# Two-layer hybrid trunk on one core: small gather, scatter and one-hot products placed inside the branch blocks, some GpSimd weight splits moved to VectorE, the second tile's input norm rewritten

## The chip, the cores and the metric

One core of one Trainium2 chip runs the whole program. The metric is device microseconds (us) of one execution, the median of several runs. Lower is better. Everything below stands in us unless it says otherwise.

## The reference, cut to what matters

Two layers over 256 tokens of width 1024, all fp32. Each layer is a token mixer and a channel mixer, each followed by a layer norm of `alpha * x + f(x)`. The channel mixer of the first layer is a dense SwiGLU, that of the second a mixture of eight experts:

```python
x = layer_norm(x, ln_emb_g, ln_emb_b)
for l in range(2):
    x = layer_norm(DN_ALPHA * x + hybrid_mixer(x, w_in[l], ...), ln1_g[l], ln1_b[l])
    f = swiglu(x, ...) if l == 0 else moe_swiglu(x, router, w_gate, w_up, w_down)
    x = layer_norm(DN_ALPHA * x + f, ln2_g[l], ln2_b[l])

def moe_swiglu(x, w_router, w_gate, w_up, w_down):   # w_gate, w_up: 8 x 1024 x 3584, w_down: 8 x 3584 x 1024
    top_v, top_i = lax.top_k(xt @ w_router, 2)
    top_w = jax.nn.softmax(top_v, axis=-1)
    gates = jnp.sum(one_hot(top_i, 8) * top_w[..., None], axis=1)
    for e in range(8):
        y = y + gates[:, e:e + 1] * swiglu(xt, w_gate[e], w_up[e], w_down[e])
```

## The kernel before, in words

**Weights.** Every weight arrives as fp32 and is split on the chip into a high part `whi` (a ScalarE copy, L151) and a low part `wlo` (the difference, L152, on VectorE or, where a list says so, on GpSimd). A product of two fp32 matrices is then three TensorE products, high by high, high by low, low by high (`mm3`, L161 to L163). `split` (L147) makes one such pair; `hold_splits` (L155) fills a list that says for each of the next splits on which engine its low part runs and after which instruction it may be issued.

**Start.** The 256 tokens are two tiles of 128. `norm` (L1242) does the input layer norm of a tile in four VectorE instructions of 128x512 (two at L1247, two at L1250). The first tile is normed and transposed, then the second by `second` and `third`, which hang on the split numbers in R1 = (0, 1) and on START, the list of splits whose low part is on GpSimd. NEXT is the same list for the second layer's mixer.

**Experts** (`moe`, L637). An expert takes only the tokens routed to it: a matrix of ones and zeros `pm` picks them, at most 128 rows per expert. The gather products `gx` (L741) multiply the token tiles by `pm` and are copied to `xg` in high and low parts; experts go in pairs. The result of an expert goes back by scatter products `sc` (L993, L994), which VectorE adds to the rows `r` (L999). Between the two stand `gsb` (L800, L802), which turn `pm` over and pick the gate weights, copied by ScalarE to `gs` and `pTm` (L805, L806).

The hidden width 3584 is cut into seven chunks of 512. One iteration is one (expert e, chunk m) and has three stages on TensorE: gate (`eg`, 24 products of 128x512), up (`eg`, 24) and, for the chunk before, down (`y`, 24). After the gate stage the last chunk's hidden values are transposed (`ht`, L166) and copied to `wk`, high part by ScalarE (L943), low part by VectorE (L945); the down stage multiplies `wk` by the down weights. Each stage's weight, 1024x512, is split in two pieces of 128x2048, so there are six pairs of `whi` and `wlo` in one iteration.

**Two ways through a stage.** Expert 0 is static. For experts 1 to 7 each stage is an If (`either`, L853): with more than 64 tokens the heavy way runs 24 products, with at most 64 the light way packs high and low parts side by side and runs 16 (with a fold, L863). With this input, experts 3, 5 and 6 are heavy and 1, 2, 4 and 7 are light. The branch stands on TensorE, ScalarE, VectorE and GpSimd alike; what is called between two Ifs stands between the two branches in each engine's order.

**Chores.** The gather of the next pair (eight pieces of four products), the one-hot products of a pair (two pieces of eight) and the scatter of an expert (four pieces of two) are called chores here. They lie in a list; `point` (L824) runs one if it is due, three times per iteration: after gate, after up, after down. The chore's products are issued there and its copies or sum are put off with `defer(CHORE_N, ...)`, CHORE_N = 4, that is by two splits of 2048 columns; `msplit` (L830) calls what has come due after each split. Each chore takes one PSUM bank out of a pool of four, `acc`, two of which hold `y`.

A scheduler in the framework lays out each engine's order within a stretch between branches, so chores called at different points may come to stand next to each other.

```python
def point():
    points[0] += 1
    if chores and chores[0][0] <= points[0]:
        chores.pop(0)[1]()
...
with tc.If(few[e] == 0) as cmp:
    heavy()
with cmp.Else():
    light()
```

**Start of the experts.** The router's logits are sorted to the two best (L699 to L712), counted (`pc`, L716) and turned into positions (`posm`, L721) and `pm` (L729). Three of the first splits of expert 0 have their low part on GpSimd (the `hold_splits` line in `gather`).

Of the kernel before, what the change touches and what calls it, by code (L numbers as in the profile page):

```python
# [18 lines left out]
P = 128  # L19
# [18 lines left out]
R1, R2 = (0, 1), (0, 5)  # L38
WF = 6
HBUF = 3  # L40
NEXT = (True, False, True, False)
# [45 lines left out]
def trunk(ctx: ExitStack, tc: tile.TileContext, x, consts, mconsts, vecs, lnrows, w_in, w_uq, w_ukv, w_o,  # L87
# [59 lines left out]
    def split(src, n, lo_eng=None, to=None):  # L147
        hi, lo = to or [spl[0].tile([P, 1024], F32R, tag=t, name=t) for t in ("whi", "wlo")]
        ins, eng = plan.pop(0) if plan else ((), lo_eng)
        with after(*ins):  # L150
            last[0] = nc.scalar.copy(hi[:, :n], src)  # L151
            last[1] = (eng or nc.vector).tensor_tensor(lo[:, :n], src, hi.bitcast(F32)[:, :n], ALU.subtract)  # L152
        return hi, lo

    def hold_splits(*steps):  # L155
        plan.clear()
        for ins, eng, n in steps:
            plan.extend([(ins, eng)] * n)
# [478 lines left out]
    def moe(pool, raws2, raws3, r, gb, rw):  # L637
# [87 lines left out]
        def gather(pr):  # L725
# [5 lines left out]
            if pr == 0:  # L731
                hold_splits(((), None, 2), ((pw,), nc.gpsimd, 2), ((i1, pw), nc.gpsimd, 1), ((i1, ip), None, 3))
            xgs = [pool.tile([P, KD, P, 2], F32R, tag="xg", name="xg", bufs=3) for j in range(2)]

            def half_part(k2, hl, n=0):
                src = (xth, xtl)[hl]
                b = bank(acc, "gx")
                for kk in range(2):
                    k = 2 * k2 + kk
                    for tt in range(2):  # L740
                        nc.tensor.matmul(b[:, kk * 256:(kk + 1) * 256], src[:, tt, k * P:(k + 1) * P], pm[:, tt, :],  # L741
                                         start=(kk == 0 and tt == 0), stop=(kk == 1 and tt == 1))
# [10 lines left out]
                defer(n, copies)  # L753

            def part(k2):
                for hl in range(2):
                    half_part(k2, hl)
# [28 lines left out]
        def gather2(pr, pm):  # L786
# [10 lines left out]
            def one(j):  # L797
                b = bank(acc, "gsb")
                for tt in range(2):
                    nc.tensor.matmul(b[:, 256:264], pmf[:, tt, j * P:(j + 1) * P], gates[:, tt, :], start=(tt == 0), stop=False)  # L800
                for tt in range(2):
                    nc.tensor.matmul(b[:, tt * P:(tt + 1) * P], pmf[:, tt, j * P:(j + 1) * P], ident, start=False, stop=(tt == 1))  # L802
# [5 lines left out]
                defer(CHORE_N, copies)  # L808
# [15 lines left out]
        def point():  # L824
            points[0] += 1
            if chores and chores[0][0] <= points[0]:
                chores.pop(0)[1]()


        def msplit(raw, o, halves=False, before=None):  # L830
            t = [spl[0].tile([P, 2048], F32R, tag=x, name=x) for x in ("whi", "wlo")]
            n = 1024 if halves else 2048
            for c in range(0, 2048, n):
# [4 lines left out]
                for q in list(later):  # L838
                    q[0] -= n // 1024
                    if q[0] <= 0:  # L840
                        later.remove(q)
                        q[1]()
# [10 lines left out]
        def either(e, heavy, light):  # L853
            if few[e] is None:
                return heavy()
            with tc.If(few[e] == 0) as cmp:
                heavy()
            with cmp.Else():
                light()

# [4 lines left out]
        def gate_up(e, m, xg, part=None, mid=None):  # L865
# [12 lines left out]
            for g, w in enumerate((e_gate, e_up)):  # L878
# [25 lines left out]
                else:  # L904
                    for q in range(2):
                        four(q)
                        heavy(range(4 * q, 4 * q + 4))
                if dyn:
# [18 lines left out]
            point()  # L927
# [483 lines left out]
```

## Time and profile before

| what | value |
| --- | --- |
| median of 3 runs | 1468.8 us (1468.71 to 1469.89) |
| the profiled execution's own time | 1468.16 us |
| its span in the trace | 1466.0 us |
| TensorE busy | 1359.3 us (93%), 6927 products |
| VectorE busy | 1176.5 us (80%) |
| ScalarE busy | 997.0 us (68%) |
| GpSimd busy | 78.4 us (5%) |
| mean granted TensorE clock | 0.987 |
| weights and tokens read | 426.76 MB |

The span runs from the first to the last instruction that the trace shows; the execution's own time is 2.16 us more. Busy time counts an engine as busy while an instruction is on it; TensorE's products overlap, so two neighbours' durations add up to more than they take. "Idle before" in a row is the time in which that engine did nothing ahead of the row, with the instruction that ended the wait. The experts take the span from about 491 to 1443 us.

### The profile page before, as it was taken

The numbers are of one execution on the slowest core, as the hardware profiler recorded it, in microseconds if no ns is written. First come the engines' busy times: TensorE is split into PE (matmuls) and PEld (weight loads), VectorE is DVE, ScalarE is ACT, GpSimd is POOL, SyncE is SP. The second block draws the span as 40 slices with busy tenths as digits, with TensorE's granted clock in tenths as the row PEclk, the third lists the DMA queues.
The fourth block names the chain that finished last, engine by engine and source line by source line (L and its number), as shares of the span: only waits on it lengthen the run. The fifth ranks groups of instructions, "written<-read, shape, count | busy, mean of one in ns | idle before, by whom it ended". The sixth has DMA issues, their size and how long they took to land. (4 is left out here: it accounts for less than half of the span.)

```text
span 1466.0 us, 18597 instructions
## 1 busy us (share of the span) xinstructions
PE 1359.3 (93%) x6927; PEld 1118.0 (76%) x6927; DVE 1176.5 (80%) x1256; ACT 997.0 (68%) x1073; POOL 78.4 (5%) x113
## 2 busy tenths in 40 slices
PE   7999999999999899988989999998999999999895
PEld 6987999998987688766666677866677787787663
DVE  6577655557677788899999987898998788788996
ACT  3564444444565677788978877787986777778794
POOL 3011000004102100000000000000000000000101
PEclk9999999999999999999999999999999999999998
DMA  6733555544534699999999998899998799899980
GB/s 264 276 135 115 189 186 186 188 157 153 194 116 201 231 339 356 375 365 349 420 406 369 419 382 323 325 367 348 407 419 342 295 357 357 311 358 389 357 363 30
DMA packets 63513, 429.46 MB, mean 293 GB/s; under 512 B 7058, under 2 KB 7570, under 8 KB 15268
## 3 DMA queue, kind: packets, MB, share of 16 engines
q1 hardware_dynamic: 63364, 427.81, 76.4%
q8 instruction: 81, 1.33, 0.4%
q14 instruction: 36, 0.29, 0.1%
q0 software_dynamic: 32, 0.03, 0.0%
HBM read 426.76 MB, written 1.05 MB: 292 GB/s over the span
## 5 line engine op out<-in xcount | busy, mean ns | idle before, releaser
L152 DVE TENSOR_TENSOR wlo<-raw,whi 128x2048 fp32r<-128x2048 f32 (+4 forms) x475 | 911.0, 1939 | 158.3 <-ACT whi L151 156.7
L151 ACT CAST whi<-raw 128x2048 fp32r<-128x2048 f32 (+4 forms) x482 | 771.0, 1619 | 250.5 <-PE gu L585 44.0
L898 PE MATMUL eg<-wlo,xg 128*128 128x512 f32 x448 | 185.6, 414 | 22.1 <-DVE wlo L152 19.0
L162 PE MATMUL eg<-wlo,xg 128*128 128x512 f32 x448 | 178.0, 397 | 0.8 <-DVE wlo L152 0.3
L161 PE MATMUL eg<-whi,xg 128*128 128x512 f32 x448 | 178.6, 399 | 0.0
L897 PE MATMUL eg<-whi,xg 128*128 128x512 f32 x448 | 178.4, 398 | 0.0
L163 PE MATMUL eg<-whi,xg 128*128 128x512 f32 x448 | 176.6, 394 | 0.0
L898 PEld LDWEIGHTS eg<-wlo,xg 128*128 128x128 f32 x448 | 84.4, 188 | 70.4 <-DVE wlo L152 54.9
L971 PE MATMUL y<-wlo,wk 128*128 128x512 f32 x224 | 94.2, 421 | 17.0 <-DVE wlo L152 15.8
L162 PEld LDWEIGHTS eg<-wlo,xg 128*128 128x128 f32 x448 | 86.9, 194 | 21.5 <-DVE wlo L152 5.4
L163 PEld LDWEIGHTS eg<-whi,xg 128*128 128x128 f32 x448 | 86.7, 194 | 17.3
L584 PE MATMUL gu<-xhi,whi 128*128 128x256 f32 x352 | 99.8, 283 | 0.1
L585 PE MATMUL gu<-xlo,whi 128*128 128x256 f32 x352 | 99.7, 283 | 0.2 <-DVE xlo L224 0.2
L161 PEld LDWEIGHTS eg<-whi,xg 128*128 128x128 f32 x448 | 86.9, 194 | 16.7
L586 PE MATMUL gu<-xhi,wlo 128*128 128x256 f32 x352 | 99.6, 283 | 0.0
L897 PEld LDWEIGHTS eg<-whi,xg 128*128 128x128 f32 x448 | 84.9, 189 | 15.0 <-ACT whi L151 0.5
L971 PE MATMUL y<-whi,wk 128*128 128x512 f32 x224 | 90.3, 403 | 3.6 <-DVE wk L945 1.5
L162 PE MATMUL y<-wlo,wk 128*128 128x512 f32 x224 | 88.0, 393 | 3.6 <-DVE wlo L152 3.4
L161 PE MATMUL y<-whi,wk 128*128 128x512 f32 x224 | 87.5, 392 | 0.4 <-ACT hh L919 0.4
L163 PE MATMUL y<-whi,wk 128*128 128x512 f32 x224 | 87.3, 390 | 0.0
L971 PEld LDWEIGHTS y<-wlo,wk 128*128 128x128 f32 x224 | 44.1, 197 | 42.7 <-DVE wlo L152 36.0
L584 PEld LDWEIGHTS gu<-xhi,whi 128*128 128x128 f32 x352 | 67.6, 192 | 0.7 <-DVE xlo L224 0.3
(313 smaller groups left out, 2111.8 us busy)
## 6 DMA issues: line engine op xcount, KB each, us to landing
raw<-in_e_gate SPq DMA_DIRECT2D x112, 1024.0 KB, 7.1
raw<-in_e_up SPq DMA_DIRECT2D x110, 1024.0 KB, 7.2
raw<-in_e_down SPq DMA_DIRECT2D x108, 1024.0 KB, 7.4
raw<-in_ffn_gu SPq DMA_DIRECT2D x22, 1024.0 KB, 4.8
raw<-in_ffn_dn SPq DMA_DIRECT2D x11, 1024.0 KB, 4.7
raw<-in_w_in SPq DMA_DIRECT2D x10, 960.0 KB, 4.7
raw<-in_w_o SPq DMA_DIRECT2D x8, 1024.0 KB, 6.7
gb<-in_lnrows SPq DMA_DIRECT2D x8, 512.0 KB, 5.3
```

Of the source, the lines that this page charges most:

```text
L151: last[0] = nc.scalar.copy(hi[:, :n], src)
L152: last[1] = (eng or nc.vector).tensor_tensor(lo[:, :n], src, hi.bitcast(F32)[:, :n], ALU.subtract)
L161: nc.tensor.matmul(o, ahi, bhi, start=start, stop=False)
L162: nc.tensor.matmul(o, ahi, blo, start=False, stop=False)
L163: return nc.tensor.matmul(o, alo, bhi, start=False, stop=stop)
L584: nc.tensor.matmul(o, hi[:, cs], xhi[:, k, :], start=(g == 0 and k == 0), stop=False)
L585: nc.tensor.matmul(o, hi[:, cs], xlo[:, k, :], start=False, stop=False)
L586: nc.tensor.matmul(o, lo[:, cs], xhi[:, k, :], start=False, stop=(g == 1 and k == 7))
L897: nc.tensor.matmul(bs[g], x2, sp[k // 4][0][:, cs], start=(k == 0), stop=False)
L898: nc.tensor.matmul(bs[g], x2, sp[k // 4][1][:, cs], start=False, stop=(k == 7))
L971: nc.tensor.matmul(yb[n], h2, sp[j // 2][i][:, j % 2 * D + n * 512:j % 2 * D + n * 512 + 512], start=(m == 0 and j == 0 and i == 0), stop= ...
```

## The change

Five things change.

1. A chore now returns its products and its follow-up apart. `step` takes the place of `point`; `either` calls it once per stage and runs the products at the end of the heavy block and at the end of the light block, and puts off the follow-up by CHORE_N behind the If. Expert 0, which has no If, runs them at the end of each stage.
2. What has come due after a split is now issued after that split's two instructions (`after(last[0], last[1])` in `msplit`). Scatter chores are due two steps later, not three.
3. At the start of the experts the three splits whose low part was on GpSimd go to VectorE, and are issued after `pm`.
4. At the start of the kernel the second tile's norm is one ScalarE instruction (x * rstd - mean * rstd), one VectorE product with the scale and one VectorE sum with the shift, each 128x1024, in place of four VectorE instructions of 128x512; one small GpSimd instruction gives -mean * rstd. R1 goes from (0, 1) to (0, 3), so the second of these steps comes three splits later.
5. NEXT loses its first entry: one split of 128x832 of the second layer's mixer goes from GpSimd to VectorE.

```diff
@@ -35,10 +35,10 @@
 START = (False, True, False, True)
-R1, R2 = (0, 1), (0, 5)
+R1, R2 = (0, 3), (0, 5)
 WF = 6
 HBUF = 3
-NEXT = (True, False, True, False)
+NEXT = (False, False, True, False)
 R3 = (0, 7)
@@ -146,16 +146,17 @@
         hi, lo = to or [spl[0].tile([P, 1024], F32R, tag=t, name=t) for t in ("whi", "wlo")]
-        ins, eng = plan.pop(0) if plan else ((), lo_eng)
+        ins, eng, late = plan.pop(0) if plan else ((), lo_eng, ())
         with after(*ins):
             last[0] = nc.scalar.copy(hi[:, :n], src)
+        with after(*ins, *late):
             last[1] = (eng or nc.vector).tensor_tensor(lo[:, :n], src, hi.bitcast(F32)[:, :n], ALU.subtract)
         return hi, lo
 
     def hold_splits(*steps):
         plan.clear()
-        for ins, eng, n in steps:
-            plan.extend([(ins, eng)] * n)
+        for ins, eng, n, *late in steps:
+            plan.extend([(ins, eng, late)] * n)
 
@@ -729,17 +730,19 @@
             if pr == 0:
-                hold_splits(((), None, 2), ((pw,), nc.gpsimd, 2), ((i1, pw), nc.gpsimd, 1), ((i1, ip), None, 3))
+                hold_splits(((), None, 2), ((i1,), None, 3, ip), ((i1, ip), None, 3))
             xgs = [pool.tile([P, KD, P, 2], F32R, tag="xg", name="xg", bufs=3) for j in range(2)]
 
-            def half_part(k2, hl, n=0):
+            def half_part(k2, hl):
                 src = (xth, xtl)[hl]
                 b = bank(acc, "gx")
-                for kk in range(2):
-                    k = 2 * k2 + kk
-                    for tt in range(2):
-                        nc.tensor.matmul(b[:, kk * 256:(kk + 1) * 256], src[:, tt, k * P:(k + 1) * P], pm[:, tt, :],
-                                         start=(kk == 0 and tt == 0), stop=(kk == 1 and tt == 1))
+
+                def products():
+                    for kk in range(2):
+                        k = 2 * k2 + kk
+                        for tt in range(2):
+                            nc.tensor.matmul(b[:, kk * 256:(kk + 1) * 256], src[:, tt, k * P:(k + 1) * P], pm[:, tt, :],
+                                             start=(kk == 0 and tt == 0), stop=(kk == 1 and tt == 1))
 
@@ -750,11 +753,12 @@
 
-                defer(n, copies)
+                return products, copies
 
             def part(k2):
                 for hl in range(2):
-                    half_part(k2, hl)
+                    for f in half_part(k2, hl):
+                        f()
 
@@ -821,10 +827,11 @@
 
-        def point():
+        def step():
             points[0] += 1
             if chores and chores[0][0] <= points[0]:
-                chores.pop(0)[1]()
+                return chores.pop(0)[1]()
+            return (lambda: None), (lambda: None)
 
@@ -839,7 +846,8 @@
                     q[0] -= n // 1024
                     if q[0] <= 0:
                         later.remove(q)
-                        q[1]()
+                        with after(last[0], last[1]):
+                            q[1]()
             return t
@@ -851,12 +859,14 @@
 
 
         def either(e, heavy, light):
-            if few[e] is None:
-                return heavy()
+            products, then = step()
             with tc.If(few[e] == 0) as cmp:
                 heavy()
+                products()
             with cmp.Else():
                 light()
+                products()
+            defer(CHORE_N, then)
 
@@ -905,6 +915,9 @@
                         heavy(range(4 * q, 4 * q + 4))
+                    products, then = step()
+                    products()
+                    defer(CHORE_N, then)
                 if dyn:
@@ -924,7 +937,6 @@
 
-            point()
             if e == 0 and m == 0:
@@ -990,13 +1005,19 @@
             b = bank(acc, "sc")
-            nc.tensor.matmul(b, pT[:, tt, :], y[0], start=True, stop=False)
-            nc.tensor.matmul(b, pT[:, tt, :], y[1], start=False, stop=True)
-            if last:
-                ln_sum(ya[tt], ya[tt], {n: b}, fsums[tt], 1.0, (n,))
-            else:
-                cs = slice(n * 512, (n + 1) * 512)
-                defer(CHORE_N, lambda: nc.vector.tensor_tensor(ya[tt][:, cs], ya[tt][:, cs], b, ALU.add))
+
+            def products():
+                nc.tensor.matmul(b, pT[:, tt, :], y[0], start=True, stop=False)
+                nc.tensor.matmul(b, pT[:, tt, :], y[1], start=False, stop=True)
+
+            def add():
+                if last:
+                    ln_sum(ya[tt], ya[tt], {n: b}, fsums[tt], 1.0, (n,))
+                else:
+                    cs = slice(n * 512, (n + 1) * 512)
+                    nc.vector.tensor_tensor(ya[tt][:, cs], ya[tt][:, cs], b, ALU.add)
+
+            return products, add
 
@@ -1107,14 +1129,14 @@
                         for tt in range(2):
-                            chores.append((points[0] + 3, lambda n=n, tt=tt: scatter(n, tt, ys[n], pT)))
+                            chores.append((points[0] + 2, lambda n=n, tt=tt: scatter(n, tt, ys[n], pT)))
 
         def prepare_scatter(pr):
             one = []
 
             def first():
                 one.append(gather2(pr, half[pr][0]))
-                one[0](0)
+                return one[0](0)
 
@@ -1136,7 +1158,6 @@
                 def mid():
-                    point()
                     if prev is not None:
@@ -1153,7 +1174,6 @@
                     finish(*prev[:2], ht[0], fold_up, e, hook if (e, m) == LAST else None)
-                point()
                 if m == 3 and e == NE - 1:
@@ -1250,11 +1270,16 @@
 
+
             def second(i):
-                with after(last[1]):
-                    norm(1, mv1)
+                xr = pre.tile([P, D], F32, tag="xr1", name="xr")
+                xres.append(xr)
+                with after(last[0]):
+                    nc.scalar.activation(xr, xin[1], AF.Identity, bias=mv1[:, 2:3], scale=mv1[:, 3:4])
+                nc.vector.tensor_tensor(xr, xr, t[0], ALU.mult)
 
             def third(i):
+                nc.vector.tensor_tensor(xres[1], xres[1], t[1], ALU.add)
                 with after(i):
@@ -1263,6 +1288,7 @@
             mv1 = stats(1)
+            nc.gpsimd.tensor_scalar(mv1[:, 2:3], mv1[:, 0:1], mv1[:, 3:4], -1.0, ALU.mult, ALU.mult)
             split_T(pts, 0, xhi, xlo)
```

The follow-ups of `gather2` and the static branch of `down` are changed in the same manner as `half_part` and the static branch of `gate_up`.

TensorE, expert 3, from the end of a gate stage to the first product of the up stage, before. `ht` are the transposes, `gx` the gather products, the branch rows the edges of the If:

```order
L897 MATMUL eg<-whi,xg 128x512
L898 MATMUL eg<-wlo,xg 128x512
L856 UNCONDITIONAL_BRANCH
L166 MATMUL ht<-mc,hh 128x128 x4
L741 MATMUL gx<-pm,xth 128x256 x4
L741 MATMUL gx<-pm,xtl 128x256 x4
L741 MATMUL gx<-pm,xth 128x256 x4
L856 COMPARE_AND_BRANCH
L161 MATMUL eg<-whi,xg 128x512
```

The same place after the change (the light block's end is the one shown; the heavy block, which stands ahead of it, ends with the same four `gx`):

```order
L907 MATMUL eg<-whi,xg 128x512
L908 MATMUL eg<-wlo,xg 128x512
L744 MATMUL gx<-pm,xtl 128x256 x4
L863 UNCONDITIONAL_BRANCH
L167 MATMUL ht<-mc,hh 128x128 x4
L863 COMPARE_AND_BRANCH
L162 MATMUL eg<-whi,xg 128x512
```

Three chores stood in a row between the blocks; now one stands at the end of each block and between the blocks there are only the transposes.

ScalarE, an iteration of expert 1 with chores, around the down stage's two splits, before (`fl` is the fold's copy, `wk` the copy of the transposes):

```order
L856 UNCONDITIONAL_BRANCH
L151 CAST whi<-raw 128x2048
L943 CAST wk<-ht 128x4x128
L876 CAST fl<-eg 128x512
L151 CAST whi<-raw 128x2048
L856 UNCONDITIONAL_BRANCH
```

And after the change:

```order
L863 UNCONDITIONAL_BRANCH
L151 CAST whi<-raw 128x2048
L886 CAST fl<-eg 128x512
L151 CAST whi<-raw 128x2048
L955 CAST wk<-ht 128x4x128
L863 UNCONDITIONAL_BRANCH
```

`wk` has moved behind the fold's copy and a split of 2048 columns. In iterations without chores this order is as it was.

VectorE, start of the experts, from `posm` on, before:

```order
L721 SCALAR_TENSOR_TENSOR posm<-sel,pc 128x16
L763 TENSOR_REDUCE cmax<-pc 128x1
L729 TENSOR_SCALAR pm<-mc,posm 128x128 x4
L152 TENSOR_TENSOR wlo<-raw,whi 128x1024
L749 CAST xg<-gx 128x256 x2
L765 CAST cint<-cmax 128x1
L772 TENSOR_SCALAR w_5195<-ex 128x2
L773 RECIPROCAL w_5195<-w_5195 128x2
L749 CAST xg<-gx 128x256 x2
```

And after:

```order
L722 SCALAR_TENSOR_TENSOR posm<-sel,pc 128x16
L767 TENSOR_REDUCE cmax<-pc 128x1
L730 TENSOR_SCALAR pm<-mc,posm 128x128 x4
L153 TENSOR_TENSOR wlo<-raw,whi 128x1024
L752 CAST xg<-gx 128x256 x2
L153 TENSOR_TENSOR wlo<-raw,whi 128x1024
L752 CAST xg<-gx 128x256 x4
L153 TENSOR_TENSOR wlo<-raw,whi 128x1024 x2
L752 CAST xg<-gx 128x256 x2
```

The three splits that GpSimd had now stand between the copies of the gather, and the small instructions for the gate weights (`cint`, `w`) have moved behind them.

## Rows read from the trace of the kernel before

**Rows 1.** Stretches: length, busy us (count) per engine, granted clock; plain light, plain heavy iteration.

```profile
696.43:710.83 14.40, 13.48 (x55) 9.49 (x54) 14.40 (x9) 12.97 (x10) 0.00 (x0) 1.00 1.01 420
1269.95:1287.02 17.07, 17.07 (x77) 14.17 (x76) 14.86 (x8) 13.38 (x11) 0.00 (x0) 1.00 0.93 348
```

**Rows 2.** Stretches, iterations with chores of the light experts 1, 2, 4 and 7.

```profile
627.48:696.43 68.95, 58.30 (x258) 43.82 (x257) 65.47 (x50) 55.14 (x49) 0.00 (x0) 1.00 0.97 357
740.10:777.37 37.27, 30.34 (x134) 22.36 (x133) 33.76 (x26) 27.81 (x25) 0.00 (x0) 1.00 0.94 376
982.64:1020.50 37.86, 31.45 (x133) 23.45 (x132) 34.34 (x26) 27.82 (x25) 0.00 (x0) 0.95 0.91 340
1353.03:1387.22 34.19, 28.45 (x117) 20.41 (x116) 33.62 (x22) 27.29 (x21) 4.47 (x2) 1.00 0.94 348
```

**Rows 3.** Stretches, iterations with chores of the heavy experts 3, 5 and 6.

```profile
853.12:933.60 80.48, 76.16 (x346) 61.77 (x344) 65.38 (x49) 55.71 (x49) 0.00 (x0) 1.00 0.86 329
1096.26:1176.65 80.39, 76.07 (x345) 61.67 (x344) 65.38 (x49) 55.70 (x49) 0.00 (x0) 1.00 0.85 326
1228.51:1269.95 41.44, 38.89 (x178) 31.24 (x177) 32.66 (x21) 27.33 (x25) 0.00 (x0) 1.00 0.85 308
```

**Rows 4.** Timeline, TensorE, expert 3: three chores in a row (start, us).

```profile
892.46 0.71 PE L741 MATMUL gx<-pm,xth 128*128 128x256 f32 x4
...
895.60 0.71 PE L741 MATMUL gx<-pm,xth 128*128 128x256 f32 x4 [0.94 <-DVE xg L749]
896.15 0.40 PE L161 MATMUL eg<-whi,xg 128*128 128x512 f32 x1
```

**Rows 5.** Timeline, VectorE, the same place.

```profile
894.70 0.76 DVE L749 CAST xg<-gx 128x256 fp32r<-128x256 f32 x2 [3.25 <-PE gx L741]
895.70 2.29 DVE L152 TENSOR_TENSOR wlo<-raw,whi 128x2048 fp32r<-128x2048 f32 x1 [0.24 <-ACT whi L151]
```

**Rows 6.** Timeline, TensorE, a plain heavy iteration: transposes, then the down stage's first product.

```profile
933.60 0.60 PE L166 MATMUL ht<-mc,hh 128*128 128x128 f32 x4
...
939.64 0.39 PE L161 MATMUL y<-whi,wk 128*128 128x512 f32 x1
```

**Rows 7.** Timeline, start of the experts: GpSimd, then VectorE, then TensorE.

```profile
474.53 8.20 POOL L152 TENSOR_TENSOR wlo<-raw,whi 128x1024 fp32r<-128x1024 f32 x3 [5.08 <-ACT whi L151]
...
474.69 1.20 DVE L152 TENSOR_TENSOR wlo<-raw,whi 128x1024 fp32r<-128x1024 f32 x1
...
476.02 2.12 DVE L701 SCALAR_TENSOR_TENSOR eq<-lg,v,mc 128x8 f32<-128x8 f32 x1
...
478.37 2.08 DVE L707 TENSOR_SCALAR s<-eq,m 128x8 f32<-128x8 f32 x1
480.36 2.38 DVE L701 SCALAR_TENSOR_TENSOR eq<-lg,v,mc 128x8 f32<-128x8 f32 x1
...
483.11 0.22 DVE L701 SCALAR_TENSOR_TENSOR eq<-l,v,mc 128x8 f32<-128x8 f32 x1
...
483.84 0.17 PE L716 MATMUL pc<-sel,utb 128*128 128x8 bf16 x1 [5.39 <-DVE sel L711]
```

**Rows 8.** Stretch from the first split behind pm to the last gather product.

```profile
485.81:493.87 8.06, 8.06 (x45) 7.51 (x46) 4.67 (x21) 2.85 (x7) 0.00 (x0) 0.80 0.51 194
```

**Rows 9.** Timeline, start of the kernel: GpSimd, VectorE, TensorE.

```profile
14.64 4.40 POOL L152 TENSOR_TENSOR wlo<-raw,whi 128x832 fp32r<-128x832 f32 x2 [1.03 <-ACT whi L151]
...
8.46 1.41 DVE L1247 SCALAR_TENSOR_TENSOR xr<-r,xmv,gb 128x512 f32<-128x512 f32 x2 [2.65 <-DMA gb<-in_lnrows]
...
14.75 4.84 DVE L1247 SCALAR_TENSOR_TENSOR xr<-r,xmv,gb 128x512 f32<-128x512 f32 x2
...
21.91 0.72 PE L162 MATMUL pj<-wlo,xhi 128*128 128x416 f32 x1 [3.79 <-DVE wlo L152]
```

**Rows 10.** Timeline, second layer's first split on GpSimd, then TensorE's first product of it.

```profile
329.06 1.98 POOL L152 TENSOR_TENSOR wlo<-raw,whi 128x832 fp32r<-128x832 f32 x1 [180.16 <-ACT whi L151]
...
341.18 0.35 PE L161 MATMUL pj<-whi,xhi 128*128 128x416 f32 x1
```

More of the change, by code (lines that the diff above doesn't have):

```diff
@@ L798, in one @@
                 b = bank(acc, "gsb")
[L799 to L802, printed above, removed]
+                def products():
+                    for tt in range(2):
+                        nc.tensor.matmul(b[:, 256:264], pmf[:, tt, j * P:(j + 1) * P], gates[:, tt, :], start=(tt == 0), stop=False)
+                    for tt in range(2):
+                        nc.tensor.matmul(b[:, tt * P:(tt + 1) * P], pmf[:, tt, j * P:(j + 1) * P], ident, start=False, stop=(tt == 1))
                 def copies():
@@ L806, in copies @@
                     nc.scalar.copy(pT[:, j, :, :], b[:, 0:256].rearrange("p (a b) -> p a b", b=P))
-                defer(CHORE_N, copies)
+                return products, copies
             return one
@@ L980, in down @@
                     heavy((2 * q, 2 * q + 1))
+                products, then = step()
+                products()
+                defer(CHORE_N, then)
             if fold_up and fe != e and few[fe] is not None:
@@ L992, in scatter, with products @@
             b = bank(acc, "sc")
-            nc.tensor.matmul(b, pT[:, tt, :], y[0], start=True, stop=False)
-            nc.tensor.matmul(b, pT[:, tt, :], y[1], start=False, stop=True)
-            if last:
-                ln_sum(ya[tt], ya[tt], {n: b}, fsums[tt], 1.0, (n,))
-            else:
-                cs = slice(n * 512, (n + 1) * 512)
-                defer(CHORE_N, lambda: nc.vector.tensor_tensor(ya[tt][:, cs], ya[tt][:, cs], b, ALU.add))
+            def products():
+                nc.tensor.matmul(b, pT[:, tt, :], y[0], start=True, stop=False)
[7 more added lines that the diff above has]
+            return products, add
         def ln_rows_bc2():
@@ L1097, in finish @@
                         for tt in range(2):
-                            scatter(n, tt, ys[n], pT, True)
+                            for f in scatter(n, tt, ys[n], pT, True):
+                                f()
                 else:
@@ L1124, in first @@
                 half[pr] = gather(pr)
-                half[pr][3](0, 0, CHORE_N)
+                return half[pr][3](0, 0)
             chores.append((0, first))
-            chores.extend((0, lambda i=i: half[pr][3](i // 2, i % 2, CHORE_N)) for i in range(1, 8))
+            chores.extend((0, lambda i=i: half[pr][3](i // 2, i % 2)) for i in range(1, 8))
         for e in range(NE):
```

## The prediction

> **What bounds the kernel now.** I read the shares first, then stretches of single iterations, then the timeline where a stretch is longer than its neighbours. TensorE is busy 93% of the span, VectorE 80%, and a mean over the whole says little, because two kinds of iteration have two different limits. A plain light iteration takes 14.40 us, and VectorE is busy for 14.40 of them: it is the bound, TensorE has about 0.9 us to spare. A plain heavy one takes 17.07 us and TensorE is busy for 17.07 of them, VectorE for 14.86 [rows 1]. So each kind has a floor of its own: VectorE's work in a light expert, TensorE's products in a heavy one.
>
> Iterations with chores stand above that floor. In the light experts the stretches [rows 2] take 68.95, 37.27, 37.86 and 34.19 us, VectorE being busy 65.47, 33.76, 34.34 and 33.62: it is idle for 3.48 + 3.51 + 3.52 + 0.57 = 11.1 us. In the heavy ones [rows 3] I subtract plain iterations and the chores' own products. Four gather products take 0.55 us from the first to the product after them (895.60 to 896.15 [rows 4]); I count a scatter chore like that and a one-hot chore, with twice the products, as 1.1. Expert 3: 80.48 - 4 x 17.07 - 12 x 0.55 = 5.6. Expert 5: 80.39 by the same, 5.5. Expert 6: 41.44 - 2 x 17.07 - 4 x 0.55 - 2 x 1.1 = 2.9. Together 14.0, and with the light ones **25.1 us** in which chores cost more than their work.
>
> Why they do is seen in one place [rows 4]: three gather chores in a row last from 892.46 to 896.15, 3.69 us for 3 x 0.55 = 1.65 us of products, and the third waits 0.94 us for VectorE's copy `xg` to free its bank. That copy is late for a reason of the same queue: VectorE had itself been idle 3.25 us before it, waiting for the product, and the split behind it (2.29 us) started only after it, at 895.70 [rows 5]. TensorE waits for the copies, the splits wait behind the copies, and later products wait for the splits.
>
> **The chores inside the blocks (change 1 and 2).** Removed are the places where two or three chores meet: each block now ends with one. The same 58 chores remain (28 scatter, 24 gather, 6 one-hot pieces behind expert 0), so their products and copies cost what they did; they are issued in both ways but run in one. Branches are no more than before: an iteration has the same three, and a plain heavy iteration with three of them has TensorE busy for all of its 17.07 us [rows 1], so a branch by itself costs nothing to speak of. A chore's bank is free when its copy is done, two splits behind its block; a stage of 24 products takes 17.07 / 3 = 5.7 us and two spare banks take turns, so there are some 11 us from a product to the next one into the same bank, against two splits of 2.29 and one copy of 0.38 [rows 5]. Scatter chores come due one step sooner; what they read is scaled two splits behind the expert's last block, so a stage before they are due. That is why I expect nearly all of the 25.1 to come back.
>
> What it may add: in iterations with chores, `wk` is copied behind the fold's copy and a split, on ScalarE and then VectorE. The down stage needs `wk` 6.0 us after the transposes (933.60 to 939.64 [rows 6]) in a heavy expert; a split takes 2.29, so one split of delay is covered and two would not be, by little. In a light expert a stage is 14.40 / 3 = 4.8 us and TensorE has slack, but VectorE may idle for ScalarE's half. The trace doesn't show this order. Bounds: no wait at all, or 0.9 us (a wait as the one in [rows 4]) in each of the 20 iterations with chores, 18 us lost, 7 left. I take 24: about 1 us lost. If products at a block's end cost only what the stage's own do (17.07 / 72 = 0.237 us for 512 columns [rows 1], so 0.47 in place of 0.55 for four of 256), the 32 such units of the heavy experts give 2.6 more, some 28 in all. So **-24**, from -7 to -28.
>
> **The start of the experts (change 3).** Beside GpSimd's three splits (474.53 to 482.7) three VectorE instructions on 128x8 took 2.12, 2.08 and 2.38 us, where the same kind takes 0.22 behind them [rows 7]. They stand on the chain to `posm`, `pm` and the gather, and TensorE waited 5.39 us ahead of `pc` for it. Without the splits they give back 1.90 + 1.86 + 2.16 = 5.9. Added are three splits of 1.20 us on VectorE [rows 7], 3.6, between the gather's copies. From the first split behind `pm` to the last gather product VectorE was busy 4.67 of 8.06 us [rows 8], so 3.4 of the 3.6 can stand in its idle time; of that not all lies right. I take 0.9 on the path: **-5**. Ends: all hidden, -5.9; all on the path, -2.3.
>
> **The start of the kernel (change 4).** Beside GpSimd's two splits (14.64 to 19.04) VectorE's two norm instructions took 4.84 us, alone 1.41 [rows 9]; then two more and the third split's low part, for which TensorE waited 3.79 us. Now one product of 128x1024, which I count as a split of that size, 1.20 [rows 7], stands ahead of that low part, the sum behind it. No row shows a plain product beside these splits. If it is held like the norm instructions, it ends at about 14.64 + 2.2 + 1.2 = 18.0, the low part, held by GpSimd's second split until 19.04, at about 20.1 in place of 21.9: -1.8; held by both, -0.7. If it isn't held, all of TensorE's 3.79 goes. Ends 0 and -3.8; I take **-1.5**, because the nearest row is the held one. The Trainium skill (SBUF — State Buffer, "Who interferes with whom") says that a VectorE instruction with two SBUF inputs, the plain product too, contends with a GpSimd instruction that reads SBUF, and that the later of the two waits out the whole of the other. By that rule plain instructions escape nothing and the sum would take -0.7 to -1.8 here; by a reading that blames the norm's own form it would take -3.8.
>
> **The second layer's split (change 5)** costs and brings **0**: GpSimd had it done at 331.0, ten us before TensorE's first product of that mixer at 341.18 [rows 10], which waits for the layer norm; 1.03 us on VectorE lie in that same wait. If that cover were gone, it would cost those 1.03.
>
> **Sum** against the profiled execution's own 1468.16: -24 - 5 - 1.5 = -30.5, so 1437.7. That execution lay 0.6 below the median of 1468.8, so **1438** is the forecast for the median. About 0.2%, 2.9 us, is what a measurement of this kernel can tell from no change.
>
> **Rivals.**
>
> *The light half is not recovered.* VectorE is the bound there, and a `wk` whose ScalarE half stands behind a split may hold VectorE as long as the chores did. For it: ScalarE is busy 55.14 of 68.95 [rows 2], more than a little. Against it: VectorE, not ScalarE, set the light period. Only 14 of the heavy experts, then: 1468.8 - 14 - 6.5 = 1448.
>
> *The entry is not recovered.* The three splits on VectorE delay `xg` and the expert's first products as much as the freed chain gives: 1468.8 - 24 - 1.5 = 1443, or 1447 if they cost their 3.6 on top.
>
> *The waits move, not go.* The chores inside the blocks still wait for banks and splits, now at a block's end, in the same amount. For it: the copies stay behind two splits, and the third chore's wait in [rows 4] was for such a copy. Against it: they no longer follow one another. Only the entries are left: 1468.8 - 6.5 = 1462.
>
> *Slower: every chore in a heavy block waits out a split.* A product at a block's end stops the branch and so the next block; between the blocks it could be put aside by the scheduler. If the copy that frees its bank ends after the second block behind, each of the 30 chores of experts 3, 5 and 6 waits one split of 2.29 [rows 5]: 69 in place of the heavy 14, 1468.8 + 69 - 14 - 11 - 6.5 = 1506. It decides where two splits and a copy (5 us) exceed two stages (11 us); the rows are far from it.
>
> *Transfers.* A plain light iteration already ran at 420 GB/s with the DMA share at 1.01 [rows 1], the highest of these stretches. Chores gave the queues time to run ahead (340 to 376 in [rows 2]); faster chore iterations take some of it away. If that binds in the light experts, it ends near the first rival, 1448.
>
> *It does nothing.* The order says that the products stand in the blocks, but if the waits were caused by the copies' own work and not by the order, and the entries refill: 1468.
>
> **Chances.** Forecast 0.62; light half not recovered, by either way, 0.13; entry not recovered 0.07; waits move 0.09; nothing 0.04; slower 0.05. Faster by over 0.2%: 0.62 + 0.13 + 0.07 + 0.09 = 0.91. Within 0.2%: 0.04. Slower: 0.05. The range's low end takes the best ends, 1468.8 - 28 - 5.9 - 3.8 = 1431. The high end has to hold the first two rivals and the forecast's bad ends: 1468.8 - 10 - 2.3 - 0 = 1456.5, where 10 lies between the forecast's bad end for the chores, 7, and the 14 of the first rival. It leaves out the last three, 0.18. Range 1431 to 1457.
>
> **What would show it.** In the changed trace: chore iterations of heavy experts with a stretch equal to TensorE's busy time, near 4 x 17.07 + 6 = 74.9 for expert 3 (measured 80.48); VectorE always busy in the light ones, 65 to 66 for expert 1's four; no gap ahead of `gx` or `sc`; the 128x8 instructions at the start of the experts at 0.2 us and no 5.39 ahead of `pc`; TensorE's 3.79 at the start near 2. I am wrong if products at a block's end wait for a copy, if `y` waits for `wk`, or if gaps ahead of TensorE named `raw` (transfers) appear in the light experts.

## The result and the profile after

The changed kernel takes 1434.5 us (median of four runs, 1433.8 to 1436.0) against 1469.4 for the kernel before, a ratio of 0.9764 with a 95% interval of 0.9747 to 0.9781. Forecast were 1438, 1431 to 1457. The profiled execution took 1434.80 us by itself, 33.4 less than the one of before (1468.16), and its span is 33.1 shorter.

The page of the changed kernel, the header and the busy times:

```profile
span 1432.9 us, 18660 instructions
PE 1355.6 (95%) x6927; PEld 1121.2 (78%) x6927; DVE 1171.8 (82%) x1258; ACT 999.5 (70%) x1074; POOL 68.3 (5%) x110
```

TensorE's busy time fell by 3.7 us only; the other 29.4 of the 33.1 are time in which it no longer waits. Where the 33.1 us went is read by taking the same product in both traces and comparing its start (`pj` are products of a mixer's input weights, `wo` of its output weights, `fo` of the first layer's last weights):

| product | before | after | difference so far |
| --- | --- | --- | --- |
| first `pj` | 14.37 | 13.09 | -1.28 |
| 83rd `pj` (start is over) | 50.24 | 48.12 | -2.13 |
| last `pj`, second layer's mixer | 432.41 | 430.23 | -2.18 |
| 110th `wo`, the same mixer | 444.80 | 445.49 | +0.69 |
| last router product | 474.71 | 475.03 | +0.32 |
| first `eg` of expert 0 | 488.28 | 482.25 | -6.03 |
| last `eg` | 1438.67 | 1404.55 | -34.12 |
| last `y` | 1450.10 | 1416.91 | -33.19 |

The 1.28 stand ahead of all that was changed and are luck (the first tile's norm began when its scale rows had landed, 7.39 against 8.46; when the changed kernel was run again as `f0_after_again`, its first `pj` came at 14.59). So: start -0.85, entry of the experts -6.35, experts **-28.1**. Against it stand two stretches in which nothing was changed: from the last `pj` of the second layer's mixer to its 14th `wo` (+2.87), and the last down stage (+0.93). The experts of the kernel before run from 488.28 to 1438.67, a little earlier than was said above.

The view of stretches, iterations with chores of the light experts 1, 2, 4, 7 and the heavy experts 3, 5, 6, answering to [rows 2] and [rows 3]:

```profile
621.16:684.96 63.80, 58.54 (x258) 43.88 (x257) 63.80 (x44) 55.85 (x50) 0.00 (x0) 1.00 0.99 389
729.72:763.13 33.41, 30.24 (x133) 22.39 (x132) 33.41 (x22) 28.34 (x25) 0.00 (x0) 1.00 0.99 401
962.49:995.92 33.43, 30.22 (x133) 22.39 (x132) 33.43 (x22) 28.33 (x25) 0.00 (x0) 1.00 0.97 374
1319.72:1353.12 33.40, 29.07 (x118) 20.48 (x117) 33.40 (x22) 27.30 (x21) 4.47 (x2) 1.00 0.95 368
838.81:913.35 74.54, 74.53 (x345) 62.46 (x344) 64.65 (x44) 56.10 (x50) 0.00 (x0) 1.00 0.96 358
1071.58:1146.13 74.55, 74.54 (x345) 62.47 (x344) 64.66 (x44) 56.11 (x50) 0.00 (x0) 1.00 0.94 357
1198.04:1236.31 38.27, 38.14 (x177) 31.67 (x176) 33.59 (x22) 27.80 (x25) 0.00 (x0) 1.00 0.95 340
```

After the stretch's two ends stands its length, then the first pair is TensorE, the third VectorE. In the light experts VectorE is now busy for the whole of each stretch, in the heavy ones TensorE is, but for 0.13 us in expert 6: both floors of the prediction are reached. The DMA share (the number ahead of the last) of the light stretches went from 0.91 to 0.97 up to 0.95 to 0.99, and ScalarE's waits for `raw` did not grow with it (6.6 us for the down weights over the experts, 7.3 before).

TensorE in expert 3, a gate stage's end with its chore, answering to [rows 4], and VectorE there, answering to [rows 5]:

```profile
875.70 0.64 PE L744 MATMUL gx<-pm,xtl 128*128 128x256 f32 x4
876.18 0.60 PE L167 MATMUL ht<-mc,hh 128*128 128x128 f32 x4
876.53 0.49 PE L162 MATMUL eg<-whi,xg 128*128 128x512 f32 x1
```

```profile
875.72 2.29 DVE L153 TENSOR_TENSOR wlo<-raw,whi 128x2048 fp32r<-128x2048 f32 x1 [1.18 <-ACT whi L151]
877.93 0.75 DVE L752 CAST xg<-gx 128x256 fp32r<-128x256 f32 x2
878.60 2.29 DVE L153 TENSOR_TENSOR wlo<-raw,whi 128x2048 fp32r<-128x2048 f32 x1
```

A gather chore now takes 0.48 us (875.70 to 876.18) without a bracket of idle time, and VectorE's copy finds its product done, where it had waited 3.25 us.

### The profile page after: what moved, and what is told of

The parts are those of the page before. It is cut to its first block, busy times and chain, and to the rows that moved or that the text cites. A ratio compares the mean times of both kernels' runs of the same rounds, so it can differ in the third digit from the quotient of the medians.

```text
span 1432.9 us, 18660 instructions
## 1 busy us (share of the span) xinstructions
PE 1355.6 (95%) x6927; PEld 1121.2 (78%) x6927; DVE 1171.8 (82%) x1258; ACT 999.5 (70%) x1074; POOL 68.3 (5%) x110
## 5 line engine op out<-in xcount | busy, mean ns | idle before, releaser
L153 DVE TENSOR_TENSOR wlo<-raw,whi 128x2048 fp32r<-128x2048 f32 (+5 forms) x479 | 917.1, 1935 | 163.8 <-ACT whi L151 161.7
L586 PEld LDWEIGHTS gu<-xlo,whi 128*128 128x128 f32 x352 | 67.5, 192 | 0.6 <-DVE xlo L225 0.4
```

The lines of the kernel that those rows point to most:

```text
L586: nc.tensor.matmul(o, hi[:, cs], xlo[:, k, :], start=False, stop=False)
```

## Experiments

The changed parts were first taken apart, then the reason for the largest of them. Three theories were put first: A, that chores lost time because they met between the blocks (the prediction's); B, that part of the gain hangs on the entry of the experts and the clock; C, that the new order of the follow-ups did it.

**The parts alone.** `c1_chores_only` is the changed kernel with the start's norm, R1, NEXT and the entry's `hold_splits` as before; `c2_all_but_chores` is the kernel before with just those changed.

```diff
-R1, R2 = (0, 3), (0, 5)
+R1, R2 = (0, 1), (0, 5)
...
-NEXT = (False, False, True, False)
+NEXT = (True, False, True, False)
...
-                hold_splits(((), None, 2), ((i1,), None, 3, ip), ((i1, ip), None, 3))
+                hold_splits(((), None, 2), ((pw,), nc.gpsimd, 2), ((i1, pw), nc.gpsimd, 1), ((i1, ip), None, 3))
...
```

> Changes 1 and 2 alone; start, entry of the experts and the second layer's split as before. Theory A (the gain is that chores no longer meet between the blocks): the stretch from expert 0's first product to the end of the experts shrinks by the 27.8 us that the changed kernel's trace shows there, so 27 to 28 us below the kernel before, near 1441 to 1442, with up to 3 us either way where the clock's dips fall elsewhere. Rival B (the entry's splits and the clock set the experts' start, and part of the chores' gain hangs on that): under 22 us, 1447 or more.

Measured: 1443.3 us, ratio 0.9809 (0.9789 to 0.9829), 26.6 us below the kernel before beside it (1470.0); from the first to the last `eg` 28.2 us fewer.

> Changes 3, 4 and 5 without the chores' changes: the complement. Theory A: from the traces 1.1 us at the start and 6.35 at the entry of the experts come, and 2.9 go in the second layer's mixer, where TensorE's granted clock was at half for 6.7 us; if that dip comes again 1464.8, if not 1462; chore iterations as long as before (80.5 us for expert 3's four). Rival B: chore iterations shrink too, 1450 or less.

Measured: 1462.3 us, ratio 0.9947 (0.9928 to 0.9965), 7.7 us below. Expert 3's chore iterations take 80.4 us, as before. The two parts add up to the whole (26.6 + 7.7 against 34.8), so B falls.

**The place of the products.** `c3_between` calls the chore's products ahead of the If:

```diff
             products, then = step()
+            products()
             with tc.If(few[e] == 0) as cmp:
                 heavy()
-                products()
             with cmp.Else():
                 light()
-                products()
             defer(CHORE_N, then)
```

> The changed kernel with the products called ahead of the If instead of in both ways; the follow-ups stay put off as in the changed kernel. The order on TensorE then shows up to three gather pieces between two blocks again. Theory A: they wait for one another as before, expert 3's four chore iterations take near 80 us in place of 74.5, and the kernel is 17 to 28 us slower than the changed one, 1452 to 1462. Rival C (the gain is from the follow-ups issued behind the split's two instructions and the earlier scatter, not from the place of the products): 1435 to 1438.

Measured: 1435.9 us, ratio 0.9761 (0.9743 to 0.978): as fast as the changed kernel. Three gather pieces do stand in a row again, and it costs next to nothing: expert 3's stretch is 75.0 us against 74.5. **Theory A falls.** `c4_no_after` takes away the rule that was C's candidate:

```diff
-                        with after(last[0], last[1]):
-                            q[1]()
+                        q[1]()
```

> The changed kernel without the rule that what has come due is issued behind the split's two instructions. Theory A: products stay in the blocks, one by one, so the time stays within 3 us of the changed kernel, 1433 to 1438; the copy wk is back ahead of the split. Rival C: most of the chores' gain goes, 1450 or more.

Measured: 1431.2 us, ratio 0.974 (0.9717 to 0.9763), 1.8 below the window of A and far from C's, the experts iteration by iteration as in the changed kernel: the rule does nothing more once the products are in the blocks, and `wk` stays where the changed kernel has it. **Theory C falls** as the only cause: either the place of the products or the rule will do. What the fast kernels have in common is the place of the chores' copies and sums on VectorE. In the kernel before all 52 of these instructions (28 sums `r`, 24 copies `xg`) stand between a stage's two splits, in all of the fast ones behind both. VectorE of the kernel before, expert 3:

```profile
873.28 0.69 DVE L999 TENSOR_TENSOR r<-r,sc 128x512 f32<-128x512 f32 x1 [1.01 <-PE sc L994]
873.88 2.28 DVE L152 TENSOR_TENSOR wlo<-raw,whi 128x2048 fp32r<-128x2048 f32 x1
...
880.87 0.76 DVE L749 CAST xg<-gx 128x256 fp32r<-128x256 f32 x2 [1.91 <-PE gx L741]
881.55 2.28 DVE L152 TENSOR_TENSOR wlo<-raw,whi 128x2048 fp32r<-128x2048 f32 x1
```

Each time VectorE is idle for a product of TensorE, 1.01 and 1.91 us, and the split starts right behind the copy. ScalarE waits in the same way. All waits of the two engines for a chore's product ahead of a copy or a sum, in the kernel before, from 520 to 1405 us (engine, line, released by; us in total, times, longest):

```profile
DVE xg L749 <- PE gx L741: 19.8, 11, 3.2
ACT gs L805 <- PE gsb L802: 13.7, 3, 5.7
ACT xg L751 <- PE gx L741: 12.4, 3, 4.6
DVE r L999 <- PE sc L994: 9.3, 13, 1.2
```

That is 55.2 us in 30 waits. In the same stretch of the changed kernel, of c1 and of c4 there is none, in c3 0.8 us. On ScalarE half of the changed kernel's gather copies still stand between two splits, but their products are done by then, and none waits.

That gave theory D: a copy between the two splits makes VectorE wait until TensorE has come to the chore's product, and the second split, needed half a stage later, starts only then. It was tried from both sides. `c7_before_behind_split` is the kernel before with the rule alone, products between the blocks:

```diff
                     if q[0] <= 0:
                         later.remove(q)
-                        q[1]()
+                        with after(last[0], last[1]):
+                            q[1]()
```

> The kernel before with one thing added: what has come due after a split is issued behind that split's two instructions. Products stay between the blocks, up to three gather pieces in a row; copies and sums stand behind both splits of a stage on VectorE in place of between them. Theory D (the loss is in the copies' place: a copy between a stage's two splits holds the second split until TensorE reaches the product): nearly the whole gain of the chores, 25 to 28 us, 1441 to 1446. Theory A (the loss is in the products' place between the blocks): no more than 5 us, 1464 or more.

Measured: 1448.4 us, ratio 0.9836 (0.9819 to 0.9852), 23.6 us below; from the first to the last `eg` 25.6 us fewer. The median lies 2.4 above D's window, which was drawn for a kernel before of 1469.4; beside this one it ran at 1472.0, and against that the gain is 1.4 short of the 25 forecast. Three gather pieces in a row in its trace, TensorE, and VectorE behind them:

```profile
890.51 0.63 PE L741 MATMUL gx<-pm,xth 128*128 128x256 f32 x4
890.98 0.64 PE L741 MATMUL gx<-pm,xtl 128*128 128x256 f32 x4
891.99 0.62 PE L741 MATMUL gx<-pm,xth 128*128 128x256 f32 x3 [0.37 <-ACT xg L751]
892.45 0.40 PE L161 MATMUL y<-whi,wk 128*128 128x512 f32 x1
```

```profile
897.80 2.29 DVE L152 TENSOR_TENSOR wlo<-raw,whi 128x2048 fp32r<-128x2048 f32 x1 [1.75 <-ACT whi L151]
...
900.61 0.75 DVE L749 CAST xg<-gx 128x256 fp32r<-128x256 f32 x2
```

A clump of the same three pieces as in [rows 4] takes 1.94 us in place of 3.69, and no copy or sum waits for a chore's product any more (520 to 1405 us). The rule moves everything else that is put off too, `wk` for one, but ScalarE's waits ahead of `wk` hardly change (33.8 us over the experts, 38.6 before). Whether VectorE's or ScalarE's share of the 55 us cost more was not separated. `c8_in_block_copies_between` does the opposite: products in the blocks one by one, copies back between the splits (CHORE_N 2, and the split behind a copy is issued after it):

```diff
-HT_N, CHORE_N = 4, 4
+HT_N, CHORE_N = 4, 2
...
-        with after(*ins):
+        with after(*ins, *held):
             last[0] = nc.scalar.copy(hi[:, :n], src)
-        with after(*ins, *late):
+        with after(*ins, *late, *held):
...
-                            nc.vector.tensor_copy(o, bv[:, :, j * P:(j + 1) * P])
+                            held.append(nc.vector.tensor_copy(o, bv[:, :, j * P:(j + 1) * P]))
...
```

> The changed kernel, products one by one in the blocks as there, but the copies and sums are put back between the two splits of the next stage: each comes due after one split, and the next split is issued behind it. Theory D: 12 to 28 us of the gain are lost, 1446 to 1462, and VectorE is idle ahead of xg and r. Theory A: 1433 to 1438, as the changed kernel.

Measured: 1493.0 us, ratio 1.0144 (1.0125 to 1.0163): all of the gain lost and 21 us more. The list of waits over the experts, those for chores (engine, line, released by; us in total, times, longest):

```profile
ACT xg L756 <- PE gx L746: 50.2, 12, 4.9
ACT gs L814 <- PE gsb L811: 25.5, 6, 4.9
DVE r L1022 <- PE sc L1015: 13.2, 16, 1.2
DVE xg L754 <- PE gx L746: 6.5, 6, 2.2
```

ScalarE stands still up to 4.9 us ahead of a gather copy with the stage's second `whi` behind it. The direction is D's; the size is beyond its 12 to 28 us of loss. The copies stand between the two splits on both engines, as in the kernel before, but here ScalarE waits 75.7 us for them in place of 26.1, and VectorE 19.7 in place of 29.1. My reading, not tried, is that a product at the end of a block comes later than one ahead of it.

**The rival that ended slower.** `d1_late_copies` keeps the changed kernel and holds each bank a stage longer:

```diff
-HT_N, CHORE_N = 4, 4
+HT_N, CHORE_N = 4, 8
```

> The changed kernel with CHORE_N 8 in place of 4: a bank is freed a stage later, and some copies stand between splits, but of a stage in which their product is long done. Theory D: no idle time ahead of them, 1433 to 1440. Slower rival of the prediction (a product at a block's end waits for its bank): products wait for the copies, each up to 2.3 us in the 30 blocks of the heavy experts, 1450 or more.

Measured: 1473.4 us, ratio 1.0012 (0.9998 to 1.0025): by the ratios 36 us worse than the changed kernel, a miss for D's expectation. Its list of waits:

```profile
PEld ht L167 <- DVE r L1018: 25.5, 7, 4.3
PE ht L167 <- DVE r L1018: 22.5, 7, 3.9
PE ht L167 <- DVE xg L752: 8.4, 3, 3.4
```

It is the bank, as the rival had it, but not the chore's product that waits: the transposes `ht` take a bank from the same pool (`acc`) and come first in line, up to 3.9 us. TensorE's 30.9 us are most of the 40.4 by which its experts are longer than the changed kernel's; the rest is not traced. The copies' place has a window, then: behind the two splits of the next stage it is right, between them it holds the second split, a stage later it holds the transposes.

**GpSimd at the start.** `d2_start_no_gpsimd` puts the start's two remaining GpSimd splits on VectorE:

```diff
-START = (False, True, False, True)
+START = (False, False, False, False)
```

> The changed kernel with all of the start's four splits on VectorE. In the changed kernel's trace the plain product of the second norm took 2.02 us and the third split 2.77 beside GpSimd's splits, where 1.2 and 1.03 are what they take alone. Held by GpSimd: both are back at 1.2 and 1.03, at a price of two splits of 1.03 more on VectorE; TensorE's products behind the start (the second layer of pj) come 0.5 to 2 us sooner, 1432 to 1434. If the two were not held by GpSimd: 0 to 2 us later, 1435 to 1437.

Measured: 1429.3 us, ratio 0.9707 (0.9691 to 0.9723), 2.7 below the lower window. Between the first and the 83rd `pj` 3.8 us went; about 1.7 of them are a dip of the granted clock, 3.4 us at half from 19.5 us on in the changed kernel, that this trace does not have. VectorE at the start, first of the changed kernel, then of this one:

```profile
14.89 2.02 DVE L1279 TENSOR_TENSOR xr<-xr,gb 128x1024 f32<-128x1024 f32 x1 [0.90 <-ACT xr L1278]
16.83 2.77 DVE L153 TENSOR_TENSOR wlo<-raw,whi 128x832 fp32r<-128x832 f32 x1
```

```profile
15.53 1.22 DVE L1279 TENSOR_TENSOR xr<-xr,gb 128x1024 f32<-128x1024 f32 x1
16.67 1.02 DVE L153 TENSOR_TENSOR wlo<-raw,whi 128x832 fp32r<-128x832 f32 x1
```

Without GpSimd's splits beside them the same two instructions take 0.80 and 1.75 us less. The Trainium skill (SBUF — State Buffer, "Who interferes with whom") says that a VectorE instruction with two SBUF inputs contends with a GpSimd instruction that reads SBUF, and that the later one waits for the whole of the other. The trace agrees: in the changed kernel GpSimd's splits ran from 13.79 to 15.82 and from 16.49 to 18.71, and the two end 1.09 and 0.89 us after those ends, about what they take alone (1.22 and 1.02).

The three last ran side by side, five runs each: the changed kernel again, this one again, and one with no weight split on GpSimd at all (NEXT all False besides).

> The changed kernel once more, beside the two below on the same chip: 1432 to 1437.

> The kernel with all of the start's splits on VectorE, once more. Its trace put TensorE's products after the start 3.8 us earlier than the changed kernel's, 1.7 of it from a dip of the granted clock at 19 us that was not there. If both hold over the runs, 3 to 5 us below the changed kernel beside it; if the dip comes and goes by itself, 1 to 3 below.

> The same, and the second layer's one split that was left on GpSimd on VectorE too: no weight split on GpSimd at all. There GpSimd's split of 1.98 us held a norm instruction with two SBUF inputs (2.57 in place of 1.28 us) ahead of TensorE's transposes, which waited 0.75 for the norm. Held-port reading: 0 to 1.5 us below the kernel above, since a split of 1.03 comes onto VectorE and 1.29 goes; if GpSimd's split is only the bystander: 0 to 1 us above it.

Measured: 1433.6 us (0.9741, 0.9721 to 0.9761), 1430.2 (0.9719, 0.9699 to 0.974) and 1428.2 (0.9719, 0.9693 to 0.9744). The norm instruction in the second layer took 2.57 us in the changed kernel and takes 1.28 in f1:

```profile
340.41 2.57 DVE L193 SCALAR_TENSOR_TENSOR xr<-r,sums,gb 128x1024 f32<-128x1024 f32 x1
...
335.96 1.28 DVE L193 SCALAR_TENSOR_TENSOR xr<-r,sums,gb 128x1024 f32<-128x1024 f32 x1
```

The medians go the way that the held reading says, 3.5 and 5.4 us below the changed kernel beside them, and the first of them came twice. The intervals of all three overlap; that the last beats the second is not shown. In the traces the start's gain is there both times, 35.03 to 31.23 us between the first and the 83rd `pj` (d2) and 34.91 to 30.81 (f3 against f0). The dip at 19 us is in neither, nor in f1, but it was missing in c8 too, which has the splits on GpSimd (33.10 us), so that removing them ends it is not shown. The last split's own part is 0.5 us: from the first layer's last `fo` to the 41st `pj` behind it f1 takes 11.72, all others 12.18 to 12.22.

## Why the prediction came out right, step by step

**Floors and their size.** Right. The 25.1 us of [rows 2] and [rows 3] came back and 3 more. From the first `eg` of each expert to the next's, the heavy ones gave 14.8 (14.0 forecast; expert 3's stretch 74.54 against 74.9), where products at a block's end took 0.48 us, near the 0.47 of the low bound; the light ones gave 13.0 (11.1 forecast), and what the 1.9 more are stays open. Expert 1's stretch is 63.80 and not 65 to 66, because four `pm` and two copies of VectorE lie outside it now. I kept back 1 us for `wk`; TensorE did wait for VectorE's `wk` 8.4 us in eight places, which I had named as a sign of being wrong, but in light experts, where VectorE is the bound, so it cost nothing that can be seen. The term of -24 measured -28.1 in the trace and -26.6 by itself (c1). The size was read off idle time and floors, whatever emptied them, so it could come right with a wrong cause.

**Why they come back.** Wrong, as the prediction put it: "Removed are the places where two or three chores meet". c3 and c7 leave them there and are fast, c8 has one chore to a block and is slow. The reading beside it, that VectorE stood idle 3.25 us for a product with a split behind it [rows 5], was the cause and not a companion. What putting the products in the blocks did was to move the copies: in VectorE's order they stand behind both splits then, with the rule of change 2 and without it (c4). Why the scheduler lays them there was not tried; my reading is that it takes the product to be done only with the end of its block. The rule alone does the same with the products outside, for 24 of the 27. That the change held two ways to move the copies, one in change 1 and one in change 2, was luck: the prediction counted on neither.

**The copies' bank.** Right in that no product waited for a bank, but the 11 us were too many: they left out the transposes, which take a bank of the same two once in an iteration. With three chores and the transposes an estimate from [rows 1] is 17.07 x 2 / 4 = 8.5 us from one use to the next. Two splits and a copy, 5 us, fit. d1 shows the other side: four splits and a copy, 4 x 2.29 + 0.7 = 9.9 us, would have fitted 11, but the bank comes too late.

**Entry of the experts.** Right in kind, 5 forecast, 6.35 measured (6.7 in c2). VectorE in the changed kernel, beside no GpSimd split:

```profile
476.69 0.20 DVE L702 SCALAR_TENSOR_TENSOR eq<-lg,v,mc 128x8 f32<-128x8 f32 x1
...
477.52 0.22 DVE L708 TENSOR_SCALAR s<-eq,m 128x8 f32<-128x8 f32 x1
477.65 0.22 DVE L702 SCALAR_TENSOR_TENSOR eq<-lg,v,mc 128x8 f32<-128x8 f32 x1
```

The 2.12, 2.08 and 2.38 of [rows 7] are 0.2 each. The 0.9 kept for the added splits was not used, and TensorE's clock added something: the granted clock had been 0.50 from 482.2 to 489.0 and is 1.00 here, where the wait of 5.39 us ahead of `pc` is gone. It was low there for as long in c1 and c7, which keep that wait, and in none of the ten traces without it. The view of stretches, before and after:

```profile
482.20:489.00 6.80, 3.87 (x19) 3.62 (x19) 5.70 (x28) 2.31 (x6) 0.52 (x1) 0.50 0.82 318
```

```profile
476.70:484.00 7.30, 5.89 (x40) 5.32 (x41) 6.78 (x33) 5.56 (x10) 0.00 (x0) 1.00 0.73 287
```

**Start.** -1.5 forecast, -0.85 measured, within the held reading's -0.7 to -1.8; TensorE's wait of 3.79 is 2.37 (near 2 was forecast). **Second layer's split**: 0 forecast; between the last `fo` of the first layer and that mixer's 41st `pj` the two traces shift by 0.01 us against each other.

**Not in the sum.** The clock in the second layer's mixer and in the last down stage, 3.8 us lost, and the early landing, 1.3 us won. The terms that were forecast gave 0.85 + 6.35 + 28.1 = 35.3 us in the trace in place of 30.5; that the total lies nearer to the forecast than they do is luck. The rival "light half not recovered" and the transfers fall with the light stretches, "entry not recovered" with the entry, "the waits move" with the chores' waits, of which none is left.

## What to carry to other kernels

A copy out of PSUM blocks its own engine's queue until TensorE has made what it copies: look at what stands behind the copy, and give it a place behind the work that TensorE needs next, but not so late that the bank is missed. Where a scheduler sets the order, look at every engine's order after a change, not only at the engine whose instructions were moved. Before crediting a change's stated idea, run the half of it that leaves the idea out.

## What the runs showed of the hardware that was not expected

TensorE's granted clock falls to half for stretches at places that come and go with nothing changed there. The second layer's mixer, the same work, in the kernel before and the changed one:

```profile
438.20:444.20 6.00, 5.87 (x37) 4.85 (x37) 3.63 (x22) 2.77 (x10) 0.18 (x1) 1.00 0.00 0
```

```profile
436.00:442.00 6.00, 6.00 (x21) 4.98 (x22) 1.93 (x10) 0.97 (x4) 0.00 (x0) 0.50 0.00 0
```

With 1.00 TensorE began 37 products in 6 us, with 0.50 it began 21. In both it had been through the same retention products (`rs`) ahead of it, without a wait longer than 0.3 us. That is the +2.87 of the table. In c1, c2, c3, c7, c8 and d1 the clock was low in that mixer for as long (6.8 us) as in the changed kernel, in c4, d2 and f0 for half of it, in f1 and f3 not at all. The +0.93 of the last down stage is of the same kind: the clock was low there for 3.4 us in the kernel before and for 6.8 in the changed one. So one profile against one profile is good to about 3 us here, and for a term of 1 us the start of the same product has to be compared next to the place.
